# Pairs of heads on both halves of the array, and expert weights in 8 KB runs with a ring of 2048-column tiles

## The chip, the cores and the metric

The kernel runs on one core of one Trainium2 chip. The metric is the device time of one execution in microseconds (us), lower is better. A core has a matrix engine (TensorE, in the profile PE for the products and PEld for the loading of the stationary operand), VectorE (DVE), ScalarE (ACT), GpSimd (POOL) and SyncE (SP), which here issues nearly all DMAs. Sixteen DMA engines carry the data. The profile gives one execution.

## What is computed

Two transformer stacks follow each other on a sequence of 256 tokens of width 1024, in fp32. Weights and all inputs lie in DRAM.

```python
# first block: 4 layers, mixers of three kinds in turn (sparse, dilated, block attention; 12 heads of 64)
x = layer_norm(ALPHA * x + concat([mix, memory_attention]) @ w_out)
x = layer_norm(ALPHA * x + swiglu(x, w_gate_up, w_down))
# second block: 2 layers; layer 0 mixes with rwkv7 and spatial gating, layer 1 with latent attention (16 heads)
h = layer_norm_2(DN_ALPHA * h + mix)
h = layer_norm_2(DN_ALPHA * h + mem_cross_attention(h, mem))
h = layer_norm_2(DN_ALPHA * h + hier_moe(h))      # 32 experts, 2 of them for a token
# an expert: silu(x @ w_gate[e]) * (x @ w_up[e]) @ w_down[e], [1024, 512], [1024, 512], [512, 1024]
```

In the first block the mixers have queries, keys and values of 64 columns a head; memory attention has four such heads over 256 memory rows. All 32 experts' weights are read for each of the two layers, 402.7 MB of the 697 MB that the kernel moves.

## The kernel before

**Order of the work.** The program is written in order and a planner of the framework lays out each engine's instructions from it by a simulated timeline; waits on buffers and data are put in by the framework. So instructions of neighbouring steps can change places on an engine, while the order in which buffers go round is that of the program.

**Attention.** 256 tokens are two row blocks `t`. A head's query and key are transposed, so that its 64 columns lie in 64 partitions: even heads in partitions 0 to 63, odd heads in 64 to 127. A score product thus uses one half of the rows of the matrix array. `softmax_T` (L484) takes heads of one half, as many as fit into a PSUM bank of 512 columns, into one bank (`at`, two banks in all): products (L495), mask and maximum on DVE (L497), exponential with sum on ACT (L503), division on DVE (L508), then `prob_T` with transposes on PE (L517) and a copy on ACT (L519). `attn_plain` (layers 0, 2 and 3; L526) calls it for the even heads, multiplies the result with v (L548), and goes on with the odd heads. The output of a head has 64 rows, so a product with v uses one half of the array's columns. `attn_dilated` (layer 1; scores L571, transposes L587, v L597) takes head by head; `attn_mem` (all four layers; scores L611, v L618) again the even heads and then the odd ones, the scores directly through `softmax_full`. In the second block `mla` has heads of 96 partitions (also L495) and products with v (L1426) whose column half changes from head to head. A product of fp32 operands leaves two records in the trace.

**Projections.** `unit` loads raw weights in tiles of 1 MiB (`raw`), ACT copies them rounded into a tile `wh` (L283), GpSimd or, in places, DVE writes the rest into `wl` (L285), and `mac` (L300 to L302) or `projT` (L329 to L331) multiplies both. The pairs `wh`, `wl` of 512 columns come from a ring (`wtiles`, L239): twelve pairs in the first block, four in the first part of the second (pool `wp`, `NWP = 4`), eight from its first output projection on (`wp` and `wx`). A pair is free when its last product is done. `lag` (L247) sets how far the second row block's products trail, by the number of pairs.

**Experts.** The 32 experts of a layer are taken in eight groups of four (`moe_group`); each has 32 places, so a group's activations fill 128 columns. A group needs 24 tiles of 1 MiB (gate, up and down, eight each). `moe_sources` (L1742) lists them: a tile holds two experts, and of each two neighbouring rows of 512 columns (gate, up) or one row of 1024 columns (down), 4 KB in one run. In the last group the down tiles hold four experts' 512-column halves. `moe_prefetch` (from L1777) puts tiles wherever memory is free at the time, in a round of 18 (layer 0) or 20 tiles (layer 1): `own` (tile `spill`), `mem`, `mraw`, `kv`, `xT`, `raw`, and four "w" tiles, each made of two pairs of the weight ring; `moe_fill` (L1758) then loads four pieces of 512 columns into `wh` and `wl` of both pairs, as four DMAs with runs of 2 KB (L1766), and whole tiles otherwise (L1768). `products` (L1828) asks for the tiles of a step and multiplies: for gate and up two tiles, each with two experts and two of eight row chunks; the four experts write 32 rows of a bank each, so that they use a quarter of the array's columns each (L1841). The selection of the tokens is L1824, the sum into the output L1593. After group 0 the program branches on a count (`overflow`, L1644, L1645): a further round for experts with more than 32 tokens.

Of the kernel before, what the change touches and what calls it, by code (L numbers as in the profile page):

```python
# [34 lines left out]
class K:  # L35
# [187 lines left out]
    def weight_rings(self, *rings):  # L223

        self.wslots = [p for p, n in rings for _ in range(n)]
        self.wcount = dict(rings)
        self.wnext = 0
# [162 lines left out]
class First(K):  # L390
# [96 lines left out]
    def softmax_T(self, t, heads, mask, W, scale=SCALE):  # L487

        nc = self.nc
        n = len(heads)  # L490
        p = self.at((128, 512 // W, W))
        s = self.s_tile()[:, :512].rearrange("p (j w) -> p j w", w=W)
        mx = self.sm(n, tag="amx", pad=4)
        for j, (q, k) in enumerate(heads):
            nc.tensor.matmul(p[:, j, :], q, k, start=True, stop=True)  # L495
        for j in range(n):
            nc.vector.tensor_tensor_reduce(out=s[:, j, :], in0=p[:, j, :], in1=mask, scale=1.0, scalar=SENT,  # L497
                                           op0=OP.add, op1=OP.max, accum_out=mx[:, j:j + 1])
        nm = self.sm(n, tag="anm", pad=4)
        nc.vector.tensor_scalar(nm, mx, -scale, None, op0=OP.mult)  # L500
        sums = self.sm(n, tag="asums", pad=4)
        for j in range(n):
            nc.scalar.activation(out=s[:, j, :], in_=s[:, j, :], func=AF.Exp, bias=nm[:, j:j + 1], scale=scale,  # L503
                                 accum_out=sums[:, j:j + 1])
        rs = self.sm(n, tag="ars", pad=4)
        nc.vector.reciprocal(rs, sums)
        for j in range(n):
            nc.vector.tensor_scalar(s[:, j, :], s[:, j, :], rs[:, j:j + 1], None, op0=OP.mult)  # L508
        return self.prob_T(s, n, W)

    def prob_T(self, s, n, W):
# [8 lines left out]
        return PT  # L520

# [8 lines left out]
    def attn_plain(self, t, qkT, vt, mask, mixT):  # L530
# [6 lines left out]
        for b0 in range(0, 12, 8):  # L537
            oT = self.mm((128, 4, 128))
            hmax = min(12, b0 + 8)
            for h0 in range(b0, hmax, 2 * per):  # L540
                for par in range(2):
                    hs = list(range(h0 + par, min(hmax, h0 + 2 * per), 2))
                    r = slice(64 * par, 64 * par + 64)
                    PT = self.softmax_T(t, [(qkT[r, h // 2, t * 128:(t + 1) * 128], qkT[r, 6 + h // 2, 0:W]) for h in hs],
                                        mask, W)
                    for j, h in enumerate(hs):
                        for kt in range(nk):
                            nc.tensor.matmul(oT[r, (h // 2) % 4, :], vt[kt][:, h * 64:h * 64 + 64],  # L548
                                             PT[:, j * nk + kt, :], start=(kt == 0), stop=(kt == t))
# [4 lines left out]
    def attn_dilated(self, t, qkT, vt, mixT):  # L554
# [3 lines left out]
        for h in range(4):  # L558
            heads = []
            for g in range(3):  # L560
                hh = 4 * g + h
                r = slice(64 * (hh % 2), 64 * (hh % 2) + 64)
                heads.append((qkT[r, hh // 2, t * 128:(t + 1) * 128], qkT[r, 6 + hh // 2, 0:W]))
            s = self.s_tile()[:, :3 * W].rearrange("p (g w) -> p g w", g=3)
            mx = self.sm(3, tag="amx", pad=4)
            per = 512 // W
            p = None
# [1414 lines left out]
```

## Time and profile before

| | us |
|---|---|
| median of 3 timed runs (2998.13 to 3003.35) | 2998.79 |
| profiled execution | 2996.07 |
| its span, first to last instruction | 2994.2 |
| PE busy | 2661.2 (89%) |
| DVE busy | 1415.1 (47%) |
| GpSimd busy | 1023.5 (34%) |
| ACT busy | 905.3 (30%) |

Busy time of PE is that of its pipelined products, whose ends are modelled. The page cuts the span into 40 equal slices of 75 us; a digit is the busy share in tenths, and the line of GB/s is what the DMA engines moved. Where PE stands at 9 the matrix work sets the pace; where the GB/s stay at one high level, the transfers do. First block: 0 to about 1400 us; second block's layer 0: mixer and attention to about 1840, experts to 2310; layer 1: to 2517, experts to 2980.

### The profile page before, as it was taken

How to read it: one execution, taken by the hardware profiler on the slowest of the kernel's cores; microseconds unless marked ns; L12 is line 12 of the kernel's file. 1: busy time of each engine (PE TensorE's matmuls, PEld its weight loads, DVE VectorE, ACT ScalarE, POOL GpSimd, SP SyncE). 2: the span in 40 equal slices, each digit the busy share in tenths (PEclk: the TensorE clock that was granted, in tenths of full speed). 3: DMA queues.
4: the chain of work that ended last, by engine and by line, in shares of the span. 5: the costliest groups of instructions: out<-in, count | busy, mean ns of one | idle time of the engine just before them, and what ended most of it. 6: DMA issues, size and time to landing. Idle time of an engine off the chain costs nothing. (4 is left out here: it accounts for less than half of the span.)

```text
span 2994.2 us, 37225 instructions
## 1 busy us (share of the span) xinstructions
PE 2661.2 (89%) x13571; PEld 1845.7 (62%) x13571; DVE 1415.1 (47%) x3091; ACT 905.3 (30%) x1760; POOL 1023.5 (34%) x809
## 2 busy tenths in 40 slices
PE   6899999999999999999899989877786999877885
PEld 5678876888778877887788866322331776322321
DVE  8766554765566576666775664100101654100011
ACT  3454453554555435553432041000000641000000
POOL 6445571656545572655454140000000440000000
PEclk8899997999999999999999999999998999999998
DMA  6335552555445542555433167999999367999997
GB/s 203 112 125 188 180 197 71 179 187 187 142 139 194 183 161 98 169 192 168 141 101 99 71 238 273 376 403 405 403 404 390 128 229 292 368 406 403 406 403 305
DMA packets 271579, 697.48 MB, mean 233 GB/s; under 512 B 16666, under 2 KB 47504, under 8 KB 271376
## 3 DMA queue, kind: packets, MB, share of 16 engines
q1 hardware_dynamic: 265616, 676.59, 62.4%
q0 software_dynamic: 5760, 18.32, 1.8%
q8 instruction: 111, 1.82, 0.3%
q14 instruction: 92, 0.75, 0.1%
HBM read 693.80 MB, written 1.05 MB: 232 GB/s over the span
## 5 line engine op out<-in xcount | busy, mean ns | idle before, releaser
L285 POOL TENSOR_TENSOR wl<-raw,wh 128x512 fp32r<-128x512 f32 (+3 forms) x680 | 929.8, 1392 | 1314.8 <-ACT wh L283 1275.3
L283 ACT ACTIVATE wh<-raw 128x512 fp32r<-128x512 f32 (+3 forms) x972 | 596.9, 626 | 566.8 <-PE mm L301 267.9
L300 PE MATMUL mm<-wh,xh 128*128 128x512 f32 (+3 forms) x1352 | 531.8, 396 | 13.9 <-DVE w L92 8.4
L301 PE MATMUL mm<-wh,xl 128*128 128x512 f32 (+3 forms) x1352 | 526.1, 390 | 0.2
L302 PE MATMUL mm<-wl,xh 128*128 128x512 f32 (+3 forms) x1352 | 520.5, 389 | 0.0
L285 DVE TENSOR_TENSOR wl<-raw,wh 128x512 fp32r<-128x512 f32 x292 | 398.9, 1388 | 162.2 <-PE mm L301 89.8
L300 PEld LDWEIGHTS mm<-wh,xh 128*128 128x128 f32 x1352 | 260.3, 193 | 66.7 <-ACT cs L454 8.8
L301 PEld LDWEIGHTS mm<-wh,xl 128*128 128x128 f32 x1352 | 260.5, 193 | 50.6 <-DVE xl L151 2.1
L302 PEld LDWEIGHTS mm<-wl,xh 128*128 128x128 f32 x1352 | 258.7, 191 | 50.0 <-issue 0.5
L1849 ACT ACTIVATE w<-at 128x512 f32<-128x512 f32 x16 | 9.6, 597 | 847.1 <-PE at L1841 847.1
L1639 POOL TENSOR_TENSOR x<-x,gb 128x512 f32<-128x512 f32 x2 | 3.5, 1726 | 482.9 <-DVE x L1638 482.9
L1824 PEld LDWEIGHTS tp<-oh,x 128*128 128x128 f32 x512 | 125.9, 334 | 41.8 <-issue 26.5
L1824 PE MATMUL tp<-oh,x 128*128 128x128 f32 x512 | 133.9, 413 | 12.9 <-PEq L1645 9.9
L1851 DVE SCALAR_TENSOR_TENSOR w<-w,at 128x512 f32<-128x512 f32 x16 | 11.0, 688 | 262.7 <-PE at L1841 262.7
L300 PE MATMUL mm<-wh,big 128*128 128x512 f32 x352 | 134.4, 391 | 0.0
L301 PE MATMUL mm<-wh,big 128*128 128x512 f32 x352 | 133.2, 389 | 0.0
L1850 DVE SCALAR_TENSOR_TENSOR w<-w,at 128x512 f32<-128x512 f32 x16 | 11.0, 687 | 255.7 <-ACT w L1849 255.7
L302 PE MATMUL mm<-wl,big 128*128 128x512 f32 x352 | 127.1, 390 | 0.0
L1841 PE MATMUL at<-mraw,xg 128*32 128x512 f32 x432 | 90.1, 644 | 40.5 <-DMA mraw<-in_moe_w_up_dram 23.5
L1841 PE MATMUL at<-raw,xg 128*32 128x512 f32 x328 | 70.5, 661 | 26.9 <-DMA raw<-in_moe_w_up_dram 17.8
L1841 PE MATMUL at<-xh,xg 128*32 128x512 f32 x200 | 57.7, 695 | 33.5 <-DMA xh<-in_moe_w_gate_dram 16.9
L1841 PE MATMUL at<-xl,xg 128*32 128x512 f32 x240 | 69.5, 668 | 12.3 <-DMA xl<-in_moe_w_gate_dram 7.0
(579 smaller groups left out, 4239.6 us busy)
## 6 DMA issues: line engine op xcount, KB each, us to landing
raw<-in_w_gate_up_dram SPq DMA_DIRECT2D x80, 1024.0 KB, 5.2
raw<-in_w_down_dram SPq DMA_DIRECT2D x44, 1024.0 KB, 4.9
mraw<-in_moe_w_down_dram SPq DMA_DIRECT2D x31, 1024.0 KB, 18.4
mraw<-in_moe_w_gate_dram SPq DMA_DIRECT2D x28, 1024.0 KB, 18.1
raw<-in_moe_w_up_dram SPq DMA_DIRECT2D x26, 1024.0 KB, 12.9
mraw<-in_moe_w_up_dram SPq DMA_DIRECT2D x26, 1024.0 KB, 18.4
raw<-in_w_in_a_dram SPq DMA_DIRECT2D x22, 1024.0 KB, 5.2
raw<-in_moe_w_down_dram SPq DMA_DIRECT2D x19, 1024.0 KB, 12.9
```

Of the source, the lines that this page charges most:

```text
L283: nc.scalar.activation(out=hi, in_=src, func=AF.Copy)
L285: (nc.vector if on_dve else nc.gpsimd).tensor_tensor(lo, src, hi.bitcast(F32), op=OP.subtract)
L300: nc.tensor.matmul(p, xh, hi[:, a:b], start=first, stop=False)
L301: nc.tensor.matmul(p, xl, hi[:, a:b], start=False, stop=False)
L302: nc.tensor.matmul(p, xh, lo[:, a:b], start=False, stop=last)
L1639: (nc.vector if t else nc.gpsimd).tensor_tensor(xs[t][:, s], xs[t][:, s], b[:, s], op=OP.add)
L1824: nc.tensor.matmul(p[:, j, :], xs[t].rearrange("p (q k) -> p k q", k=8)[:, kc, :], O[t], start=(t == 0), stop=(t == 1))
L1841: nc.tensor.matmul(p[ss, :], x[:, ss], got[u][m * i + j], start=first, stop=last, tile_position=(0, s0))
L1849: nc.scalar.activation(out=h, in_=gu[0], func=AF.Tanh, scale=0.5)
L1850: nc.vector.scalar_tensor_tensor(h, h, 1.0, gu[0], op0=OP.add, op1=OP.mult)
L1851: nc.vector.scalar_tensor_tensor(h, h, 0.5, gu[1], op0=OP.mult, op1=OP.mult)
```

## The change

Three things are changed. In attention, the scores of a pair of calls (even and odd heads) are issued in turn into two banks (`scores`), and the products with v in turn as well (`weighted`); both softmaxes are between them. `attn_plain`, `attn_dilated` and `attn_mem` use both, `mla` only `weighted`. The weight ring of the second block hands out tiles `wq` of 2048 columns (`wquad`), each holding two pairs; the memory is the same, half as many tiles. An expert tile holds one expert, and of it four rows of 512 or two of 1024 columns, which lie next to each other in DRAM: 8 KB in one run. So a step of `products` takes four tiles with one expert each, and a "w" tile is one whole `wq` tile with one DMA. The last group's down tiles keep their layout.

```diff
-    def weight_rings(self, *rings):
+    def weight_rings(self, *rings, paired=False):
+        self.wpaired = paired
...
+        if self.wpaired:
+            if self.wnext % 2 == 0:
+                self.wtwo = self.wquad()
+            self.wnext += 1
+            return self.weight_views(self.wtwo)[1 - self.wnext % 2]
...
+    def wquad(self):
+        p = self.wslots[self.wnext % len(self.wslots)]
+        return p.tile([128, 4 * WCOLS], F32R, tag="wq", name="wq", bufs=self.wcount[p] // 2)
...
+    def scores(self, groups, W):
+        banks = [self.at((128, 512 // W, W)) for _ in groups]
+        for j in range(len(groups[0])):
+            for p, heads in zip(banks, groups):
+                self.nc.tensor.matmul(p[:, j, :], *heads[j], start=True, stop=True)
+        return banks
+
+    def softmax_T(self, groups, mask, W, scale=SCALE):
+        nc = self.nc
+        n = len(groups[0])
+        banks = self.scores(groups, W)
+        res = []
+        for p in banks:
...
+            res.append((s, sums))
+        return [self.prob_T(self.divided(s, sums, n), n, W) for s, sums in res]
...
+    def weighted(self, steps, nk):
+        for js in steps:
+            for kt in range(nk):
+                for out, v, P in js:
+                    self.nc.tensor.matmul(out, v(kt), P(kt), start=(kt == 0), stop=(kt == nk - 1))
...
-                for par in range(2):
-                    hs = list(range(h0 + par, min(hmax, h0 + 2 * per), 2))
-                    r = slice(64 * par, 64 * par + 64)
-                    PT = self.softmax_T(t, [(qkT[r, h // 2, t * 128:(t + 1) * 128], qkT[r, 6 + h // 2, 0:W]) for h in hs],
-                                        mask, W)
...
+                cs = range(h0 // 2, min(hmax, h0 + 2 * per) // 2)
+                rows = [slice(0, 64), slice(64, 128)]
+                PT = self.softmax_T([[(qkT[r, c, t * 128:(t + 1) * 128], qkT[r, 6 + c, 0:W]) for c in cs] for r in rows],
+                                    mask, W)
+                self.weighted([[(oT[r, c % 4, :], lambda kt, h=2 * c + par: vt[kt][:, h * 64:h * 64 + 64],
+                                 lambda kt, j=j, P=PT[par]: P[:, j * nk + kt, :]) for par, r in enumerate(rows)]
+                               for j, c in enumerate(cs)], nk)
...
-        pairs = [slice(gi * EG + e, gi * EG + e + 2) for e in range(0, EG, 2)]
+        ones = [slice(gi * EG + e, gi * EG + e + 1) for e in range(EG)]
         for n in ("moe_w_gate", "moe_w_up"):
-            w = A[n][l].rearrange("e (p q k) n -> q p e (k n)", q=4, k=2)
-            yield from (w[q][:, es, :] for q in range(4) for es in pairs)
-        w = A["moe_w_down"][l].rearrange("e (p k) n -> k p e n", k=4)
+            w = A[n][l].rearrange("e (p q k) n -> q p e (k n)", q=2, k=4)
+            yield from (w[q][:, es, :] for q in range(2) for es in ones)
         if gi < NG - 1:
-            yield from (w[k][:, es, :] for k in range(4) for es in pairs)
+            w = A["moe_w_down"][l].rearrange("e (p q k) n -> q p e (k n)", q=2, k=2)
+            yield from (w[q][:, es, :] for q in range(2) for es in ones)
         else:
+            w = A["moe_w_down"][l].rearrange("e (p k) n -> k p e n", k=4)
...
-                got = [[t.bitcast(F32) for _ in range(1024 // WCOLS) for t in self.wtiles()]]
+                got = [[self.wquad().bitcast(F32)]]
+                self.wnext += 2
...
-            for k in range(0, 8, 2):
-                products([(p, xg[:, k + j, :], k + j == 0, k + j == 7) for j in range(2)])
+            for k in range(0, 8, 4):
+                products([(p, xg[:, k + j, :], k + j == 0, k + j == 7) for j in range(4)])
...
-            for k in range(4):
-                products([(yp[n], hT[:, k, :], k == 0, k == 3) for n in ns])
+            for k in range(0, 4, len(ns)):
+                products([(yp[n], hT[:, k + j, :], k + j == 0, k + j == 3) for j in range(len(ns)) for n in ns])
...
-            self.weight_rings((wp, NWP))
+            self.weight_rings((wp, NWP), paired=True)
...
-                    self.weight_rings((wp, NWP), (wx, NWP))
+                    self.weight_rings((wp, NWP), (wx, NWP), paired=True)
```

## Rows read from the trace of the kernel before

**Rows 1.** The page by 40 slices: PE's busy tenths, and GB/s moved.
```profile
PE   6899999999999999999899989877786999877885
...
GB/s 203 112 125 188 180 197 71 179 187 187 142 139 194 183 161 98 169 192 168 141 101 99 71 238 273 376 403 405 403 404 390 128 229 292 368 406 403 406 403 305
```

**Rows 2.** Busy time by stretch: PE, PEld, DVE, ACT, POOL, clock, DMA share, GB/s.
```profile
1400.00:1740.00 340.00, 311.76 (x2074) 274.33 (x2073) 234.41 (x535) 101.17 (x174) 145.21 (x120) 0.95 0.36 117
...
1915.00:2308.00 393.00, 305.70 (x1473) 103.67 (x1472) 37.47 (x67) 3.58 (x6) 0.00 (x0) 0.97 1.03 402
...
2584.00:2978.00 394.00, 313.62 (x1484) 106.75 (x1484) 37.99 (x68) 3.58 (x6) 0.00 (x0) 0.94 1.02 397
```

**Rows 3.** The same view, 4 us each: 4 KB runs, then twice 2 KB runs.
```profile
2031.00:2035.00 4.00, 2.88 (x16) 0.53 (x16) 0.00 (x0) 0.00 (x0) 0.00 (x0) 1.00 1.03 410
...
2107.00:2111.00 4.00, 4.00 (x20) 1.91 (x16) 0.00 (x0) 0.00 (x0) 0.00 (x0) 1.00 1.05 389
2657.00:2661.00 4.00, 4.00 (x18) 1.88 (x14) 1.19 (x3) 0.00 (x0) 0.00 (x0) 1.00 1.05 388
```

**Rows 4.** DMA issues: count, KB each, us to landing; as many go to `wl`.
```profile
wh<-in_moe_w_up_dram SPq DMA_DIRECT2D x60, 256.0 KB, 7.0
...
wh<-in_moe_w_gate_dram SPq DMA_DIRECT2D x56, 256.0 KB, 9.3
...
wh<-in_moe_w_down_dram SPq DMA_DIRECT2D x42, 256.0 KB, 7.4
```

**Rows 5.** The page's count of DMA packets by size.
```profile
DMA packets 271579, 697.48 MB, mean 233 GB/s; under 512 B 16666, under 2 KB 47504, under 8 KB 271376
```

**Rows 6.** Timeline of SP at layer 0's branch: start, us, queue, line, what.
```profile
1891.58 2.31 SPq L1768 DMA_DIRECT2D mraw<-in_moe_w_down_dram  x1
1910.57 0.38 SPq L1768 DMA_DIRECT2D spill<-in_moe_w_gate_dram  x1
```

**Rows 7.** Timeline of PE in layer 0's attention: start, us, records.
```profile
158.30 0.72 PE L495 MATMUL at<-big 64*128 64x128 f32 x8
...
163.52 1.13 PE L495 MATMUL at<-big 64*128 64x256 f32 x4 [0.36 <-DVE amx L497]
...
165.53 1.62 PE L495 MATMUL at<-big 64*128 64x256 f32 x8
...
169.88 1.09 PE L548 MATMUL mm<-big 128*64 128x128 f32 x8
```

**Rows 8.** Timeline of PE in the latent attention: products with v.
```profile
2378.77 0.66 PE L1426 MATMUL mm<-ring,vv 128*64 128x128 f32 x8
```

**Rows 9.** Groups by line: busy us, mean ns; idle before, and what ended it.
```profile
L548 PE MATMUL mm<-big 128*64 128x128 f32 x216 | 29.4, 280 | 5.5 <-ACT big L519 5.5
L495 PE MATMUL at<-big 64*128 64x256 f32 (+1 forms) x144 | 24.2, 356 | 1.7 <-DVE big L92 1.1 <-DVE amx L497 0.5
L618 PE MATMUL mm<-big,mv 128*64 128x128 f32 x128 | 21.9, 326 | 0.7 <-ACT big L519 0.7
L611 PE MATMUL at<-mkT,big 64*128 64x256 f32 x64 | 20.3, 469 | 10.1 <-ACT big L631 9.8 <-ACT w L822 0.2
L571 PE MATMUL at<-big 64*128 64x128 f32 (+1 forms) x48 | 15.6, 500 | 3.9 <-DVE amx L572 3.6
```

**Rows 10.** Busy time by stretch: the end of layer 0's attention.
```profile
157.30:179.40 22.10, 19.08 (x133) 14.23 (x131) 17.66 (x74) 17.05 (x51) 2.38 (x2) 1.00 0.44 144
```

**Rows 11.** Groups by line, 1400 to 1850 us: the two steps of weight conversion.
```profile
L283 ACT ACTIVATE wh<-raw 128x512 fp32r<-128x512 f32 x136 | 84.0, 630 | 171.5 <-PE mm L330 66.5 <-PE mm L301 63.4 <-issue 28.0
...
L285 POOL TENSOR_TENSOR wl<-raw,wh 128x512 fp32r<-128x512 f32 x112 | 149.1, 1352 | 150.1 <-ACT wh L283 133.5 <-PE mm L302 13.5 <-issue 2.2
```

**Rows 12.** PE's waits, 1400 to 1850 us: total, times, longest; the largest for weights.
```profile
PE mm L302 <- POOL xh L285: 2.1, 2, 1.9
```

**Rows 13.** Busy time by stretch: one expert group of layer 1.
```profile
2586.00:2648.00 62.00, 46.91 (x229) 15.78 (x225) 5.46 (x11) 0.60 (x1) 0.00 (x0) 0.97 1.03 404
```

**Rows 14.** DVE's groups by shape, layer 0's attention: mask and maximum of a head.
```profile
L497 DVE CUSTOM_DVE_ANT_0 big<-at,am 128x256 f32<-128x256 f32 x12 | 4.6, 418 | 0.1
```

More of the change, by code (lines that the diff above doesn't have):

```diff
@@ new lines, in attn_dilated @@
+        per = 512 // W
+        ts = slice(t * 128, t * 128 + 128)
+        for h0 in range(0, 4, 2):
+            rows = [slice(0, 64), slice(64, 128)]
+            s = [self.s_tile()[:, :3 * W].rearrange("p (g w) -> p g w", g=3) for _ in rows]
+            mx = [self.sm(3, tag="amx", pad=4) for _ in rows]
+            for g0 in range(0, 3, per):
+                gs = range(g0, min(3, g0 + per))
+                cs = [2 * g + h0 // 2 for g in gs]
+                banks = self.scores([[(qkT[r, c, ts], qkT[r, 6 + c, 0:W]) for c in cs] for r in rows], W)
+                for i, p in enumerate(banks):
+                    for g in gs:
+                        nc.vector.tensor_tensor_reduce(out=s[i][:, g, :], in0=p[:, g - g0, :], in1=masks[g], scale=1.0,
+                                                       scalar=SENT, op0=OP.add, op1=OP.max, accum_out=mx[i][:, g:g + 1])
+            PT = [self.dilated_T(s[i], mx[i], t, W) for i in range(2)]
+            oT = self.mm((128, 4, 128))
+            parts = []
+            for r0 in range(h0 * 192, h0 * 192 + 384, 64):
+                ch, ro = divmod(r0, 128)
+                parts.append((oT[ro:ro + 64, ch % 3, :], lambda kt, r0=r0: vt[kt][:, r0:r0 + 64],
+                              lambda kt, P=PT[r0 // 192 - h0]: P[:, kt, :]))
+            self.weighted([parts[i:i + 2] for i in range(0, 6, 2)], t + 1)
+            c0 = 3 * (h0 // 2)
+            self.split(mixT[0][:, c0:c0 + 3, ts], mixT[1][:, c0:c0 + 3, ts], oT[:, 0:3, :])
@@ new lines, in dilated_T @@
+    def dilated_T(self, s, mx, t, W):
+        nc = self.nc
+        nm = self.sm(1, tag="anm", pad=4)
+        nc.vector.tensor_reduce(nm, mx, axis=AX.X, op=OP.max, negate=True)
+        nc.vector.tensor_scalar(nm, nm, SCALE, None, op0=OP.mult)
+        sm = self.sm(1, tag="asums", pad=4)
+        nc.scalar.activation(out=s, in_=s, func=AF.Exp, bias=nm, scale=SCALE, accum_out=sm)
+        rs = self.sm(1, tag="ars", pad=4)
+        nc.vector.reciprocal(rs, sm)
+        P = s[:, 0, :]
+        nc.vector.tensor_tensor(P, P, s[:, 1, :], op=OP.add)
+        nc.vector.tensor_tensor(P, P, s[:, 2, :], op=OP.add)
+        nc.vector.tensor_scalar(P, P, rs, None, op0=OP.mult)
+        tp = self.tp((128, 4, 128))
+        for kt in range(t + 1):
+            nc.tensor.transpose(tp[:, kt, :], P[:, kt * 128:(kt + 1) * 128], self.ident)
+        PT = self.pt_tile().rearrange("p (j w) -> p j w", w=128)
+        nc.scalar.activation(out=PT[:, :t + 1, :], in_=tp[:, :t + 1, :], func=AF.Copy)
+        return PT
```

117 lines of the change are left out of this document (30 added, 87 removed).

## Prediction, before the changed kernel was built or run

> **What bounds the kernel now.** I read the page by slices first, for where the kernel changes its limit. PE is at 9 tenths in nearly every slice up to two thirds of the span; then the transfers run at about 405 GB/s for two long blocks while PE falls to 7 or 8 tenths [rows 1]. The reader is to see two kernels in one: matrix work first, expert weights afterwards. The busy time by stretch settles it. From 1915 to 2308 us and from 2584 to 2978 us the DMA engines are busy all the time (a share of 1.02 to 1.03) at 402 and 397 GB/s, and PE works 306 and 314 of 393 and 394 us [rows 2]. So 787 us are paced by how fast expert weights arrive, and only faster arrival shortens them. In the matrix part, 1400 to 1740 us for one, PE works 312 of 340 us and the transfers reach 117 GB/s: there only less work or less waiting on PE counts [rows 2].
>
> **Part 1: expert weights in 8 KB runs.** Each tile of 1 MiB has 128 partitions of 8 KB. Before, such a row comes as two runs of 4 KB (two experts), or, in the tiles that lie in the weight ring, as four runs of 2 KB in four DMAs of 256 KB [rows 4]. After, it is one run of 8 KB, and one DMA. Three stretches of 4 us show the price of a run: where only 4 KB runs were under way, 410 GB/s; where only 2 KB runs were, 389 and 388 [rows 3]. A MiB (1.0486 MB) takes 1.0486/0.410 = 2.558 us by the one and 1.0486/0.388 = 2.703 us by the other. Each of the 16 engines moves 16 runs of 4 KB or 32 runs of 2 KB in that time: 159.8 and 84.5 ns each. So 2 KB more in a run cost 75.3 ns, and a run has some 9 ns of its own. Continued to 8 KB: 159.8 + 2 x 75.3 = 310.4 ns, eight of them 2.483 us, 422 GB/s. A tile gains 0.075 us against 4 KB runs and 0.220 us against 2 KB runs. This is an extrapolation by a factor of two, and the step on which most hangs.
>
> How many tiles: 393 us at 402 and 394 us at 397 GB/s are 314.4 MB or 300 tiles. The last group's eight down tiles of each layer stay in 2 KB runs, so 284 change. Of all 384 tiles, (60 + 56 + 42) / 2 = 79 went to the ring, 21% [rows 4]; of 284 that is 60. The sum is 60 x 0.220 + 224 x 0.075 = 13.2 + 16.8 = 30 us. Some tiles before these stretches gain too, but there SP issues nothing from 1893.9 to 1910.6 us, where the program branches, and the queue runs dry [rows 6]; what arrives earlier there waits, and I count 2 us for it, 32 in all. SP itself saves three of four issues per ring tile; in the steady state it stands in its own full queue (2.31 us in one issue [rows 6], about a tile's time), so that is free. Bounds: 9 us, if 8 KB runs keep the pace of 4 KB ones (60 x 0.145), to 37 us, if the earlier tiles count in full.
>
> PE now needs four tiles for a step instead of two. It runs the first pieces of the first three while it waits for the fourth, and the expert stretch from 2586 to 2648 us, one group's time, holds 46.9 us of PE work in 62 [rows 13]. A group's 24 tiles take at least 59 us after the change. I cost this at nothing, covered by those 12 us; what it costs without the cover is the third rival.
>
> **Part 2: two heads of different array halves together.** Before, the heads of one half are done, then those of the other. The timeline shows both cases, because the planned order sometimes already put two calls side by side: eight score records of 128 columns took 0.72 us, while four records of 256 columns in one half took 1.13 us alone and eight of them 1.62 us where two calls met only in part [rows 7]. For the products with v, eight records in one column half took 1.09 us [rows 7]; in the latent attention, where the halves come in turn by head, eight took 0.66 us [rows 8]. So the pairing works on this engine: a factor of 0.61 for v, and for 256-column scores about 1.2 us instead of 2 x 1.13.
>
> Plain attention (three layers): the v products hold 29.4 us and the scores 24.2 us [rows 9]. At 0.61 the first give 11.5 us; the scores, partly paired already, about 5: 16 us. But in the stretch from 157.3 to 179.4 us PE works 19.1, DVE 17.7 and ACT 17.1 of 22.1 us [rows 10]. With PE shorter, DVE is late next, and 22.1 - 17.7 = 4.4 us is the most that a layer can give; I take 3, so 9 in all. Memory attention (eight calls): 21.9 us of v products and 20.3 us of scores [rows 9], at 0.61 and 0.53 a saving of 8.5 + 9.5 = 18. It lies among projections that keep PE full, so PE time saved is time saved, but before these scores PE also stood idle 10.1 us for a bank, which stays. I take 10. Dilated attention: 15.6 us of scores [rows 9], partly paired; I take 2, with 0 and 8 as bounds. Latent attention changes only the order within a pair of v products: 1. The sum is 22 us, with 9 + 18 + 8 + 1 + 4 = 40 as the upper bound (the 4 is 3 x 4.4 less the 9).
>
> Its cost: a pair of calls needs both score banks free at once. PE then waits until DVE has masked what the second bank held: two reductions of 418 ns and their read-outs, about 1.0 us [rows 14]. There are some 29 such pairs (15 plain, 8 memory, 6 dilated), so 29 us is the bound on the loss side if nothing else is queued on PE; I take none, since projections stand behind most of these pairs and the bank was waited for before, too. The Trainium skill, page "TensorEngine Tiling (Array Packing)", section "Restrictions and Gotchas", says that different row tiles can't access one PSUM bank at the same time, so sharing one bank between the halves would not be a way around this wait.
>
> **Part 3: a ring of 2048-column tiles.** In the second half of the model four (later eight) slots become two (later four) tiles that each hold two weight pairs, and a tile is refilled only when both pairs are used up. ACT's copy into a free tile takes 630 ns, GpSimd's rest behind it 1352 ns [rows 11]; 136 pairs, 68 tiles, pass there. Queued behind a late copy on ACT are the copies of the next pairs, and PE waits for them. With single slots PE waited for weights in four places, the largest sum of 2.1 us [rows 12], at most 8.4 in all, because ACT waits 66.5 + 63.4 us for PE instead [rows 11]: the ring is full, and PE is late. Lower bound 0 (that slack covers everything); upper bound 68 x (0.63 + 1.35) = 135 us (no overlap at all). I take the value near the row that shows slack: 10 us. It is made of the six 512-column projections through four slots, where the second row block lags by two chunks: there the refill is needed just as the tile comes free, two times 1.3 us each, 16 us, of which other matrix work fills a good third.
>
> **Sum.** Against the profiled run's 2996.07 us (span 2994.2 and 1.9 around it): 2996 - 32 - 22 + 10 = 2952 us. The three timed runs have a median of 2998.79, 2.7 above the profiled run; I shift by a part of that: 2953 us.
>
> **Rivals.**
> First, 8 KB runs go no faster than 4 KB ones. For it: in a profile of 271579 packets only 203 are of 8 KB or more [rows 5], none of them weights, so no row shows the new pace. Against it: the price per byte between 2 and 4 KB is steady. Then only the ring's 60 tiles gain, 9 us: 2996 - 9 - 22 + 10 = 2975. The Trainium skill, page "DMA: Bandwidth & Descriptors", section "SWDGE vs HWDGE vs iDMA", gives a packet as preferably at most 4096 B; if that means that longer runs are cut to this size, it is this rival. The trace bears it out as far as weights go, but packets of more than 8 KB do exist.
> Second, the attention gains nothing, since DVE and ACT end its chain (17.7 and 17.1 of 22.1 us [rows 10]) or the planned order had the halves together anyway: 2996 - 32 + 10 = 2974.
> Third, PE becomes late in the expert stretches: with longer waits the granted clock (0.97 there now [rows 13]) falls to its lower level more often, and 12 us more per group eat the gain: 2996 - 22 + 10 = 2984.
> Fourth, the other side: the ring of two tiles makes PE wait. If each of the 68 refills is late by GpSimd's 1.35 us, that is 92 us: 2996 - 54 + 92 = 3034, slower. It decides from 54/68 = 0.79 us a refill on. Against it: ACT's 130 us of waiting for PE, and other chains' matrix work between the projections.
>
> **How the numbers follow.** The forecast has 0.52; the first rival 0.16, the second 0.14, the third 0.06, the fourth 0.08; 0.04 is left for a new order that evens it all out. A measurement of this kernel tells 0.2%, 6 us, from no change. The first two rivals and most of the third are faster, which with the forecast makes 0.85; 0.07 for no change, 0.08 for slower. The range goes from 2918 (37 and 40 us of gain, no cost) to 2986 (the third rival and a little): it takes in three rivals and leaves out the fourth.
>
> **What would show it.** In the changed profile: transfers at about 422 GB/s in the expert stretches (410 would be the first rival), each some 20 us shorter at most; expert issues of 1024 KB only; v products at about 0.66 us for eight records; the stretch after the first layer's projections about 3 us shorter with DVE nearly full; PE's waits for ACT's and GpSimd's weight copies of about 15 us between 1400 and 1850 us, not 90; and PE's clock in the expert stretches not below about 0.9. The prediction is wrong if the run price doesn't continue to 8 KB, or if a refill of the ring is on PE's path nearly every time.

## The result, and the profile after

The changed kernel takes 2956.6 us (median of 4 runs, 2955.75 to 2962.95) against 2999.19 us before (4 runs); the ratio is 0.986 with a 95% interval of 0.9843 to 0.9877, so 42.6 us less, 36.9 to 47.1 by the interval. The forecast was 2953 us. The profiled execution takes 2956.99 us.

The page by slices (the lines that answer to [rows 1], with the granted clock, and the count of packets that answers to [rows 5]):

```profile
PE   6899999999999998999899989888787899877885
...
PEclk8899998999999999999999999999999999999989
...
GB/s 199 121 116 188 182 199 86 188 182 191 136 145 187 184 161 115 165 177 162 150 86 103 111 164 234 399 422 421 421 421 401 177 179 280 397 421 421 421 422 307
DMA packets 201220, 697.41 MB, mean 236 GB/s; under 512 B 12874, under 2 KB 43712, under 8 KB 153920
```

The two expert blocks stand at 421 GB/s where they stood at 403 to 406. Of 201220 packets, 47300 have 8 KB or more (203 before): the runs arrive whole.

Busy time by stretch of after (us, then PE, PEld, DVE, ACT, GpSimd with their counts, granted clock, DMA share, GB/s): the matrix part of [rows 2], the two expert stretches, one expert group as in [rows 13], and the attention stretch of [rows 10].

```profile
1400.00:1740.00 340.00, 312.11 (x2044) 275.46 (x2043) 225.52 (x510) 90.14 (x163) 140.98 (x114) 0.94 0.34 113
...
1915.00:2250.00 335.00, 270.19 (x1333) 97.75 (x1333) 32.54 (x60) 2.99 (x5) 0.00 (x0) 0.94 1.01 421
2584.00:2910.00 326.00, 260.67 (x1289) 94.17 (x1287) 29.83 (x53) 3.58 (x6) 0.00 (x0) 0.93 1.01 421
...
2586.00:2648.00 62.00, 48.21 (x266) 18.95 (x266) 6.15 (x12) 0.60 (x1) 0.00 (x0) 1.00 1.01 421
...
157.30:179.40 22.10, 18.70 (x113) 12.94 (x113) 15.58 (x72) 15.03 (x47) 0.39 (x1) 0.85 0.41 133
```

In a group's 62 us PE gets through 266 records instead of 229. In the attention stretch it gets through 113 instead of 133, at a clock of 0.85 instead of 1.00: in this execution the change brought nothing there.

Both kernels have 13571 matrix records, so the start of the k-th one, counted from the first, shows where the time went. Time in before, then how far the others are ahead (minus) or behind there (three of the experiments below beside after; one profiled execution each):

```
record   before    after  attention alone  ring alone  e10_split
  2000    464.0     -0.4        -1.6           +0.3       -3.7
  2250    524.6    -10.3       -11.6           +0.3      -10.8
  6300   1399.9    -11.7       -13.0           +0.3      -12.3
  8250   1704.0     -1.4       -13.2          +13.2      -14.4
  9000   1863.7     -4.6       -13.7           +8.4      -17.1
 10750   2328.4    -21.1       -12.0           +3.5      -34.7
 11750   2516.5    -22.5       -10.0           +2.3      -35.8
 13560   2970.2    -38.5        -9.7           -3.0      -51.1
```

Four steps stand out in the column of after: 10 us won within the 60 us of the dilated layer's attention, 10 us lost again in the second block's first mixer (records 6300 to 8250), 16.5 us won in layer 0's experts and 16.0 in layer 1's. The profiled execution of before (2996.07 us) lies at the fast end of its runs (2995 to 3007 us over all that were timed), so differences of profiles come out some 4 us smaller than those of medians.

### The profile page after: what moved, and what is told of

The parts are those of the page before. It is cut to its first block, busy times and chain, and to the rows that moved or that the text cites. A ratio compares the mean times of both kernels' runs of the same rounds, so it can differ in the third digit from the quotient of the medians.

```text
span 2954.8 us, 36636 instructions
## 1 busy us (share of the span) xinstructions
PE 2623.8 (89%) x13571; PEld 1833.6 (62%) x13571; DVE 1418.1 (48%) x3091; ACT 897.8 (30%) x1760; POOL 1024.6 (35%) x809
## 2 busy tenths in 40 slices
DMA packets 201220, 697.41 MB, mean 236 GB/s; under 512 B 12874, under 2 KB 43712, under 8 KB 153920
## 5 line engine op out<-in xcount | busy, mean ns | idle before, releaser
L296 POOL TENSOR_TENSOR wl<-raw,wh 128x512 fp32r<-128x512 f32 (+1 forms) x520 | 724.1, 1418 | 604.4 <-ACT wh L294 588.7
L294 ACT ACTIVATE wh<-raw 128x512 fp32r<-128x512 f32 (+1 forms) x776 | 479.7, 628 | 326.5 <-PE mm L312 183.5
L311 PE MATMUL mm<-wh,xh 128*128 128x512 f32 (+2 forms) x1152 | 454.7, 397 | 12.9 <-DVE w L92 8.9
L296 POOL TENSOR_TENSOR wq<-raw,wq 128x512 fp32r<-128x512 f32 (+2 forms) x160 | 206.5, 1315 | 701.8 <-DMA raw<-in_mla_w_in_dram 459.7
L312 PE MATMUL mm<-wh,xl 128*128 128x512 f32 (+2 forms) x1152 | 449.6, 391 | 0.0
L313 PE MATMUL mm<-wl,xh 128*128 128x512 f32 (+2 forms) x1152 | 448.7, 391 | 0.0
L296 DVE TENSOR_TENSOR wl<-raw,wh 128x512 fp32r<-128x512 f32 x256 | 358.9, 1426 | 143.6 <-PE mm L312 90.1
L294 ACT ACTIVATE wq<-raw 128x512 fp32r<-128x512 f32 (+2 forms) x196 | 109.1, 611 | 247.3 <-issue 117.5
L1869 PE MATMUL at<-mraw,xg 128*32 128x512 f32 x432 | 120.2, 678 | 31.6 <-DMA mraw<-in_moe_w_up_dram 22.7
L1869 PE MATMUL at<-wq,xg 128*32 128x512 f32 x464 | 124.2, 662 | 26.3 <-DMA wq<-in_moe_w_up_dram 17.9
L1869 PE MATMUL at<-xl,xg 128*32 128x512 f32 x240 | 129.0, 672 | 12.8 <-DMA xl<-in_moe_w_gate_dram 8.5
```

What stands on the lines that cost most here:

```text
L294: nc.scalar.activation(out=hi, in_=src, func=AF.Copy)
L296: (nc.vector if on_dve else nc.gpsimd).tensor_tensor(lo, src, hi.bitcast(F32), op=OP.subtract)
L311: nc.tensor.matmul(p, xh, hi[:, a:b], start=first, stop=False)
L312: nc.tensor.matmul(p, xl, hi[:, a:b], start=False, stop=False)
L313: nc.tensor.matmul(p, xh, lo[:, a:b], start=False, stop=last)
L1869: nc.tensor.matmul(p[ss, :], x[:, ss], got[u][m * i + j], start=first, stop=last, tile_position=(0, s0))
```

## The experiments

### Each part alone

The prediction's sum has three parts. Each was added to the kernel before by itself; the other two stayed as they were.

**e1_attn**, the changes of `softmax_T`, `scores`, `weighted` and the four attention functions alone.

> The kernel before with the attention part alone: scores of even and odd heads in turn into two banks, products with v in turn; ring and expert tiles as before. Theory of the prediction: 22 us faster, about 2977, of it 9 in plain, 10 in memory, 2 in dilated and 1 in latent attention. Rival read from the trace of after (its progress by matrix instructions is 11.7 us ahead of before at the end of the first block, 10 of them won between the dilated layer's 464 and 515 us, none in the memory parts): 12 to 15 us faster, about 2985. Second rival: the lead in the first block comes from another order of the planner and not from the pairing: within 6 us of 2999.

Measured: 2983.07 us against 3000.4, ratio 0.9941 (0.9928 to 0.9955): 17 us less. The column above shows them nearly all in one place, the dilated layer.

**e2_runs**, `moe_sources` and the steps of `products` alone.

> The kernel before with the 8 KB runs alone: expert tiles of one expert, four tiles a step, but the ring as before, so that its 'w' tiles still come as four DMAs of 256 KB in 2 KB runs. Theory that the time goes by the length of a run: the 224 tiles outside the ring gain 0.075 us each, 17 us, the ring's 60 nothing: about 2982, and 412 GB/s in the expert stretches. Rival, the gain of after comes from the ring's tiles arriving in one DMA rather than four (fewer and larger DMAs): no gain here, about 2999 at 402 GB/s. Rival, steps of four tiles make PE late: slower than 2999.

Measured: 2986.42 us, ratio 0.9947 (0.9934 to 0.996): 14 us less where the theory of the run's length expected 17, and neither rival holds in full. The expert stretches reach 406 and 408 GB/s, not the expected 412. In the group from 2586 to 2648 us it is 397 GB/s at a DMA share of 0.99, so the transfers were not always kept going there; whether the ring's tiles in 2 KB runs or the steps of four tiles do that is not shown.

**e3_ring**, `wquad`, `paired=True` and the "w" tile as one DMA alone.

> The kernel before with the ring of 2048-column tiles alone: expert tiles of two experts in 4 KB runs as before, a 'w' tile being one ring tile with one DMA, now in 4 KB runs. Theory: the paired release costs 10 us between 1400 and 1700 us (the page after shows a lead of 11.7 us shrink to 1.4 there), and 60 tiles go from 2 KB to 4 KB runs, 9 us less: within 3 us of 2999. Rival, the shrinking lead is a matter of the attention's order or of the granted clock: 9 us faster, about 2990. Rival, the ring costs 92 us: no longer possible after the result.

Measured: 2992.71 us, ratio 0.9974 (0.9963 to 0.9984): 8 us less. That lies between the two expectations, and the table tells where: the ring loses 12.8 us between 1400 and 1700 us, as the first theory said, but about 16 come back, not 9: 13.2 us behind at record 8250, 8.4 at the start of the experts, 3.0 ahead at the end. PE's waits in that stretch (1400 to 1700 us; us in total, times, longest), first of the ring alone, then of after:

```profile
PE mm L342 <- POOL wq L296: 6.2, 13, 0.9
PE mm L340 <- ACT wq L294: 1.1, 1, 1.1
```
```profile
PE mm L342 <- POOL wq L296: 6.1, 13, 0.9
PE mm L340 <- ACT wq L294: 0.7, 1, 0.7
```

L342 is the last product of the transposed projections (L331 before), where PE had waited 1.9 and 1.5 us for `wl`, five times. By the code, `projT` takes a unit of four pairs and goes over all of them twice (f = 0, then 1). With four single slots, the next unit's first pair can be written when two chunks of the second pass are done; with two tiles only after four, and the conversion (ACT's step has a mean of 623 ns, GpSimd's of 1359 ns in after) no longer fits into what is left of the pass. This is read from the code.

These waits are the smaller part of the loss. From record 6300 to 8250, in before and then in after:

```profile
1404.15:1708.40 304.25, 284.17 (x1951) 253.25 (x1950) 207.07 (x440) 89.70 (x152) 137.32 (x112) 0.97 0.36 117
```
```profile
1392.75:1707.25 314.50, 291.32 (x1951) 258.50 (x1950) 208.38 (x440) 84.02 (x152) 138.06 (x112) 0.95 0.35 113
```

The stretch is 10.2 us longer, but PE stands idle only 3.1 us more (23.2 instead of 20.1). The other 7.2 us are PE's busy time for as many records, at a mean granted clock of 0.95 instead of 0.97. The ring alone and e8_4k, which have the same two tiles, also show 0.95 there; the attention part alone has 0.97 and e10_split 0.98. What makes the clock fall with the ring, the waits or the other order, is not shown.

### The length of a run

**e8_4k**, after with tiles of two experts again:

```diff
-            w = A[n][l].rearrange("e (p q k) n -> q p e (k n)", q=2, k=4)
+            w = A[n][l].rearrange("e (p q k) n -> q p e (k n)", q=4, k=2)
...
-            for k in range(0, 8, 4):
+            for k in range(0, 8, 2):
```

> The kernel after with expert tiles of two experts again, 4 KB in a run and two tiles a step; attention and ring as in after, a 'w' tile still one DMA. Theory that time goes by the length of a run: 410 GB/s in the expert stretches instead of 421, 284 tiles x 0.07 us = 20 us slower than after, about 2977. Rival, fewer and larger DMAs are what counts: as fast as after, 2957.

Measured: 2979.33 us, ratio to before 0.9933 (0.9919 to 0.9947), 22.7 us more than after. Tiles, DMAs and their size are those of after; only the run is half as long. The same two stretches:

```profile
1915.00:2250.00 335.00, 267.33 (x1296) 92.23 (x1296) 31.62 (x59) 2.98 (x5) 0.00 (x0) 0.94 1.03 409
2584.00:2910.00 326.00, 260.00 (x1260) 90.50 (x1258) 30.25 (x54) 2.98 (x5) 0.00 (x0) 0.94 1.03 409
```

409 to 421 GB/s is 1.0486 x (1/0.409 - 1/0.421) = 0.073 us a tile, 20.8 us for 284. It is the length of the run that counts. PE's clock is the same within 0.01, so it has no part in this.

### The ring

**e10_split**, after with single pairs in the first part, and one pool of four tiles from the first output projection on:

```diff
+            self.kv = ctx.enter_context(pool("kv"))
-            wp = ctx.enter_context(pool("wp"))
-            self.weight_rings((wp, NWP), paired=True)
+            first = ExitStack()
+            wp = first.enter_context(pool("wp"))
+            self.weight_rings((wp, NWP))
...
-                    self.weight_rings((wp, NWP), (wx, NWP), paired=True)
+                    first.close()
+                    self.weight_rings((wx, 2 * NWP), paired=True)
```

> The kernel after, with the weight ring of the second block's first part in single pairs of 512 columns again (four, in a pool that is closed when the later ring opens), and the later ring of four 2048-column tiles in one pool. Expert tiles and their 8 KB runs stay. Theory that the paired release of two tiles costs the 10 us between 1417 and 1700 us (e3_ring lost 12.8 us there by itself), and that with four tiles it costs nothing: 2946. Rival, the four tiles cost as much, or the new pool has to wait: 2954 to 2960.

Measured: 2948.05 us (2945.49 to 2951.44, 5 runs), ratio to before 0.9832 (0.9819 to 0.9845), against 0.986 for after: 8.5 us less than after by the medians, and the slowest of its runs is faster than the fastest of after. Between records 6300 and 8250 of the table nothing is lost any more (12.3 us ahead, then 14.4). PE's waits there are those of before again:

```profile
PE mm L342 <- POOL wl L296: 1.5, 3, 0.6
PE mm L342 <- DVE wl L296: 1.4, 2, 1.0
```

PE's busy time from record 6300 to 8250 is 281.6 us, less than before. So the two tiles cost what was lost there, by the waits and by the clock, and four tiles cost nothing that can be seen.

**e9_kept** tried the same in another way: a ring tile is kept for good while projections go round, and its two pairs are overwritten one by one.

```diff
-            if self.wnext % 2 == 0:
-                self.wtwo = self.wquad()
+            if i not in self.wkept:
+                self.wkept[i] = self.wquad()
```

> The kernel after, but a 2048-column ring tile is kept while projections go round and only handed over anew for an expert tile; so a pair is overwritten as soon as its own products are done, while an expert tile still arrives as one DMA in 8 KB runs. Theory that the paired release costs 8 to 10 us in the second block's first mixer: about 2947, and the waits of the transposed projections for GpSimd's rest (6.1 us in 13 between 1400 and 1850 us) go back to about 1.5. Rival, those 10 us come from the planner's order or from the clock there (0.91 against 0.96 in 1400 to 1480 us): within 3 us of 2956.

Measured: 2951.82 us, ratio 0.9838 (0.9825 to 0.985). The number decides nothing: the program asks for a unit's four pairs before the trailing row block's products with the last two pairs of the unit ahead stand in it; with a tile handed out anew they keep their own weights, with a kept tile they read the next unit's. So a part of the products is done with other weights, and with other dependences.

### The attention

**e5_dilated**, **e6_plain**, **e7_memory**: pairs of heads in one of the three functions alone, in the kernel before. The others keep the order of before, for plain attention for instance by

```diff
+                for par, r in enumerate([slice(0, 64), slice(64, 128)]):
+                    P1, = self.softmax_T([[(qkT[r, c, t * 128:(t + 1) * 128], qkT[r, 6 + c, 0:W]) for c in cs]], mask, W)
+                    self.weighted([[(oT[r, c % 4, :], lambda kt, h=2 * c + par: vt[kt][:, h * 64:h * 64 + 64],
+                                     lambda kt, j=j: P1[:, j * nk + kt, :])] for j, c in enumerate(cs)], nk)
```

> The kernel before with pairs of heads in dilated attention alone (and the turn within a pair of v products in latent attention, about 1 us); plain and memory attention as before. The prediction gave dilated attention 2 us (bounds 0 and 8). Theory now: dilated attention holds most of the 17 us that the attention part alone brought, since in the trace of before the matrix engine runs at a granted clock of 0.5 from 495 to 510 us there and the section is 10 us shorter in after: about 2989. Rival, the whole attention part is needed: within 6 us of 3000.

> The kernel before with pairs of heads in plain attention alone (layers 0, 2 and 3); dilated and memory attention as before. The prediction gave it 9 us: about 2991. Theory now: the matrix engine has less to do per softmax and falls to the lower clock in this very stretch (granted 0.50 from 170 to 175 us in after and from 165 to 170 us in the attention part alone, 1.00 all through in before), which takes the gain back: 0 to 4 us faster, about 2998.

> The kernel before with pairs of heads in memory attention alone (all four layers); plain and dilated as before. The prediction gave it 10 us, because it lies among projections that keep the matrix engine full: about 2990. Theory now: the work saved (8.7 us of v products) returns as waiting for the score banks (14.2 us idle ahead of these scores in after, 10.1 in before) and as other order: 0 to 4 us faster, about 2998.

Measured: dilated 2986.58 us, ratio 0.9954 (0.994 to 0.9967), 14 us less; plain 2998.05, 0.9992 (0.9982 to 1.0002); memory 2999.44, 0.9998 (0.9988 to 1.0008). So 14 of the 17 us come from dilated attention; the other two can't be told from nothing.

What the clock did, for plain attention: PE's busy time by stretch in layer 0, of plain alone, then of after, then of e8_4k. Before, the whole section had 1.00 [rows 10].

```profile
165.00:170.00 5.00, 5.00 (x15) 2.91 (x15) 2.78 (x17) 3.19 (x12) 0.00 (x0) 0.50 0.00 1
170.00:175.00 5.00, 5.00 (x26) 3.21 (x23) 4.06 (x20) 5.00 (x16) 0.00 (x0) 0.62 0.00 0
```
```profile
165.00:170.00 5.00, 2.91 (x21) 1.94 (x19) 5.00 (x25) 5.00 (x17) 0.00 (x0) 0.96 0.00 0
170.00:175.00 5.00, 4.97 (x26) 3.58 (x26) 3.05 (x10) 3.30 (x12) 0.00 (x0) 0.50 0.52 150
175.00:180.00 5.00, 5.00 (x33) 3.57 (x32) 0.69 (x1) 2.26 (x4) 0.00 (x0) 0.85 0.18 65
```
```profile
170.00:175.00 5.00, 3.48 (x30) 2.48 (x30) 3.84 (x11) 4.55 (x14) 0.00 (x0) 1.00 0.33 86
```

A granted 0.50 is the lower of TensorE's two levels, 1.2 GHz. The order of the records doesn't settle it: after, e8_4k and e10_split have the same first 800 matrix records in the same order (by name and shape), up to beyond this section, and in the last two the clock stays at 1.00 from 140 to 205 us. Their profiles show what plain attention gains when the clock doesn't fall. Layer 0's section (records 560 to 760) in before, in e8_4k and in after:

```profile
154.85:191.90 37.05, 34.03 (x201) 26.31 (x200) 21.07 (x79) 19.46 (x55) 4.83 (x3) 1.00 0.26 86
```
```profile
153.60:189.55 35.95, 31.83 (x202) 23.97 (x201) 21.05 (x79) 19.29 (x55) 4.87 (x3) 1.00 0.28 89
```
```profile
152.85:190.85 38.00, 34.60 (x201) 25.80 (x200) 21.00 (x79) 19.26 (x55) 4.84 (x3) 0.91 0.27 84
```

Layer 2's (records 3560 to 3760) in before and in plain alone:

```profile
817.60:853.70 36.10, 34.61 (x202) 26.79 (x201) 20.60 (x68) 18.98 (x49) 4.69 (x4) 1.00 0.28 89
```
```profile
819.30:854.55 35.25, 32.93 (x201) 24.54 (x200) 20.45 (x68) 19.14 (x49) 4.68 (x4) 1.00 0.29 91
```

PE's work falls by 2.2 and 1.7 us, the section by 1.1 and 0.9: about half of what PE saves comes back as waiting for the softmax's other steps, at full clock. Where the clock falls, layer 0's section takes 37.3 to 38.0 us (attention part alone, plain alone, after), and the rest of the gain is gone too.

The pairing itself works, as the timeline of after in this stretch shows (start, us, records): sixteen v records in 1.31 us at full clock, 0.66 for eight; but fourteen in 1.97 where the clock is low.

```profile
156.95 1.31 PE L552 MATMUL mm<-big 128*64 128x128 f32 x16
158.71 1.55 PE L504 MATMUL at<-big 64*128 64x256 f32 x8 [0.45 <-DVE amx L517]
...
171.76 1.97 PE L552 MATMUL mm<-big 128*64 128x128 f32 x14
```

Memory attention is a different matter. The groups of after (busy, mean ns, idle before):

```profile
L504 PE MATMUL at<-mkT,big 64*128 64x256 f32 x64 | 20.6, 526 | 14.2 <-ACT big L659 13.9 <-ACT w L850 0.2
L552 PE MATMUL mm<-big,mv 128*64 128x128 f32 x128 | 13.2, 291 | 0.9 <-ACT big L543 0.9
```

The v products fall from 21.9 to 13.2 us [rows 9], a factor of 0.60; the scores stay at 20.3 to 20.6, and PE waits 4 us longer for a bank. The scores of layer 0, first before, then after:

```profile
119.84 1.13 PE L611 MATMUL at<-mkT,big 64*128 64x256 f32 x4
125.91 2.98 PE L611 MATMUL at<-mkT,big 64*128 64x256 f32 x8 [4.36 <-ACT big L631]
```
```profile
119.91 1.13 PE L504 MATMUL at<-mkT,big 64*128 64x256 f32 x4
125.96 2.99 PE L504 MATMUL at<-mkT,big 64*128 64x256 f32 x8 [4.33 <-ACT big L659]
```

They are laid out as before: the program has them in turn, but the planner still puts the four of one bank ahead of the four of the other. In layers 1 and 2 the first row block's do come in turn, but the second's run in part at the lower clock. Layer 1, one line of each row block, before and then after:

```profile
439.03 1.13 PE L611 MATMUL at<-mkT,big 64*128 64x256 f32 x4
443.57 1.13 PE L611 MATMUL at<-mkT,big 64*128 64x256 f32 x4 [1.17 <-ACT big L631]
```
```profile
438.02 0.70 PE L504 MATMUL at<-mkT,big 64*128 64x256 f32 x4
443.78 2.07 PE L504 MATMUL at<-mkT,big 64*128 64x256 f32 x4 [3.25 <-ACT big L659]
```

So the unchanged sum of 20.3 to 20.6 us hides a gain and a loss.

**e11_in_turn** keeps the two heads side by side and takes the turns out of the program:

```diff
-        for j in range(len(groups[0])):
-            for p, heads in zip(banks, groups):
+        for p, heads in zip(banks, groups):
+            for j in range(len(groups[0])):
...
-            for kt in range(nk):
-                for out, v, P in js:
+        for i in range(len(steps[0])):
+            for js in steps:
+                out, v, P = js[i]
+                for kt in range(nk):
```

> The attention part alone (e1_attn), with the two heads still taken together into two banks and their softmaxes side by side, but the products not in turn: all scores of the even heads, then all of the odd ones, and the v products likewise, even heads first. Theory that the halves of the array working at the same time bring the gain: most of the 17 us is gone, 2992 to 3000. Rival, the gain is that two heads are in flight while the other engines work on one, so that the matrix engine waits less and keeps its clock: still 12 to 17 us faster than before, 2983 to 2988.

Measured: 2989.03 us, ratio 0.9966 (0.9954 to 0.9978), 12 us less than before: between the two, nearer to the rival. Dilated attention by stretch, in before, in the attention part alone (e1_attn), and in this kernel:

```profile
485.00:513.00 28.00, 25.00 (x109) 15.73 (x107) 21.17 (x90) 11.63 (x29) 2.20 (x2) 0.60 0.27 82
```
```profile
485.00:513.00 28.00, 24.24 (x130) 17.41 (x130) 14.15 (x62) 9.73 (x22) 0.00 (x0) 0.82 0.24 79
```
```profile
485.00:513.00 28.00, 23.60 (x142) 17.04 (x140) 16.52 (x70) 10.29 (x25) 1.51 (x1) 1.00 0.34 112
```

Before, this stretch ran at a mean granted clock of 0.60. With two heads in flight and no turns in the program it ran at 1.00, and this kernel wins 10.3 us on before from record 2000 to 2250. (In its trace some records of the two halves still start together, two at 464.79 us for instance.) With the turns it wins 10.0 there, at 0.82. So the program's turns are not needed for those 10 us. But the kernels also differ in clock. The whole section (records 2000 to 2250) in before, in after, in e8_4k, whose records there have the order of after, and in this kernel:

```profile
468.50:529.15 60.65, 57.65 (x252) 41.40 (x251) 30.77 (x110) 20.52 (x45) 7.59 (x6) 0.76 0.18 60
```
```profile
468.45:519.15 50.70, 46.57 (x252) 34.86 (x251) 30.00 (x113) 21.35 (x47) 7.58 (x6) 0.90 0.27 93
```
```profile
466.00:519.50 53.50, 49.52 (x252) 36.66 (x251) 30.11 (x113) 21.25 (x47) 7.57 (x6) 0.84 0.26 88
```
```profile
469.10:519.40 50.30, 45.90 (x252) 34.96 (x251) 29.88 (x111) 20.84 (x46) 7.59 (x6) 1.00 0.24 83
```

In one and the same order, 0.06 of clock makes 2.8 us. By that price, an estimate, 0.76 to 0.90 makes some 6 of the 10 us between before and after, and the order with turns would take some 46 us at 1.00, 4 less than the one without. So most of the dilated layer's gain is a higher clock; that the turns are worth something at an equal clock is likely, but no run shows it. The 6 us between the two medians can't be placed: the profiles are 3 us apart, and 2.3 of that stand at record 2000 already, ahead of the dilated layer.

**e13_twice**, to ask whether more work on PE keeps the clock up in plain attention:

```diff
+        for _ in range(times):
+            for j in range(len(groups[0])):
+                for p, heads in zip(banks, groups):
...
-                                    mask, W)
+                                    mask, W, times=2)
```

> The attention part alone (e1_attn), with every score product of plain attention issued twice, the second time over the first with the same result: added work for the matrix engine, some 12 us at full clock in three layers if the halves work together, and nothing else changed. Theory that plain attention loses its gain to the lower clock: the stretch from 155 to 185 us keeps a granted clock near 1.0, and the added work costs little, 2980 to 2987 (e1_attn: 2983). Rival, the clock there has nothing to do with how busy the engine is: the lower clock stays and the run is 8 to 14 us slower than e1_attn, 2991 to 2997.

Measured: 3015.43 us, ratio 1.0045 (1.0031 to 1.0058), 32 us slower than e1_attn and worse than the rival said. The theory has fallen:

```profile
155.00:160.00 5.00, 2.28 (x17) 1.58 (x15) 5.00 (x13) 1.82 (x3) 3.60 (x3) 1.00 0.62 189
160.00:190.00 30.00, 29.96 (x106) 22.09 (x107) 14.81 (x82) 14.25 (x53) 0.00 (x0) 0.50 0.12 39
```

After 2.76 us of waiting for DVE the clock is at its lower level for 30 us in which PE is busy all the time. Waiting alone isn't it either: before, PE worked 2.98 of the 5 us from 170 to 175 us, and the clock stayed at 1.00. Nor is the order alone: one order had both clocks (after and e8_4k above). What lets it fall in these sections stays open.

**e12_split_dilated** is e10_split with plain attention in the order of before, as in the diff above, and memory attention too:

```diff
-        banks = self.scores([[(qmT[r, j, t * 128:(t + 1) * 128], mkT[r, j, :]) for j in range(2)] for r in rows], 256)
-        PT = []
-        for p in banks:
+        for par, r in enumerate(rows):
+            p, = self.scores([[(qmT[r, j, t * 128:(t + 1) * 128], mkT[r, j, :]) for j in range(2)]], 256)
...
```

> e10_split (8 KB runs, single pairs in the first ring) with plain and memory attention head by head as before, so that only dilated attention takes heads in pairs. Theory that plain and memory attention together bring 3 us or less: 2948 to 2953. Rival, they bring the 19 us of the prediction: 2967.

Measured: 2948.2 us (2942.91 to 2951.65), ratio 0.9822 (0.9809 to 0.9836): as fast as e10_split. By their medians both are 8 us faster than the changed kernel.

## Why the prediction came out right, step by step

**What bounds the kernel: right.** The expert stretches gained with the pace of the transfers, 16.5 and 16.0 us, and the matrix part only where PE worked or waited less. One thing is missing in it: the granted clock changes what the same work costs there, and it moved both the dilated layer and the second block's first mixer by several us.

**8 KB runs: right.** Forecast 422 GB/s and 2.483 us a tile. SP's queue shows it directly, an issue every 2.48 us (timeline of SP in after):

```profile
2617.83 0.33 SPq L1793 DMA_DIRECT2D wq<-in_moe_w_gate_dram  x1
2620.32 0.33 SPq L1793 DMA_DIRECT2D xh<-in_moe_w_gate_dram  x1
2622.80 0.33 SPq L1793 DMA_DIRECT2D xl<-in_moe_w_gate_dram  x1
```

The extrapolation of 75 ns for every 2 KB of a run held at twice the length. The sum was 32 us; the trace has 32.5 in the two expert blocks (16.5 and 16.0). The first rival is out (e8_4k is slower than after by 22.7 us). The Trainium skill, page "DMA: Bandwidth & Descriptors", section "SWDGE vs HWDGE vs iDMA", gives a packet as at most 4096 B preferably, in a table on what GpSimd builds for its own DMAs. The loads here are issued by SyncE; their packets of 8 KB arrived whole and went faster, 421 against 409 GB/s, so for these loads the measurement decides against that preference.

**Pairs of heads: the sum nearly right (22 forecast, 17 measured), its terms wrong.** Plain attention was given 9 us and brought 2 or nothing. The step that failed is that PE's shorter work would end the stretch earlier, up to DVE's 17.7 us, by 3 us a layer. At full clock the sections of layers 0 and 2 got 1.1 and 0.9 us shorter for 2.2 and 1.7 us less work: the rest came back as waits in the chain of a softmax, which DVE's busy time doesn't show. In after and two other kernels the clock also fell in layer 0, which the row of before at 1.00 [rows 10] couldn't show; e8_4k and e10_split show that it need not. Memory attention was given 10 and brought 1 or nothing: its v products shrank as forecast (0.60 against 0.61), its scores not at all in sum, because the planner kept the old order in layers 0 and 3 and part of the others ran at the lower clock, and PE waited 4 us longer for banks, a wait that was costed at nothing. Eight score records of 256 columns in turn took 1.40 to 1.55 us at full clock, not the 1.2 of the prediction. Dilated attention was given 2 and brought 14: the mean of 500 ns a record [rows 9] was read as the price of the work, though much of it ran at the lower clock. With two heads in flight the clock was higher, with the turns (0.90 over the section) and without them in the program (1.00, e11_in_turn); by the estimate above some 6 of the 10 us there are the clock's, a term the prediction didn't have.

**The ring: the size right (10 forecast, 10.3 in after, 12.8 alone), by luck.** The forecast was some 15 us of PE waiting for the copies in the projections of 512 columns, a third of it filled. PE's waits for the copies come to 7.8 us (6.1 + 1.0 + 0.7, 1400 to 1850 us), where before had 6.5 (2.1 + 1.9 + 1.5 + 1.0), and most of them lie in the transposed projections. All of PE's idle time grew by 3.1 us; the other 7.2 are busy time of as many records at a lower mean clock, which the prediction had no term for. The argument that ACT's 130 us of waiting for PE are slack was no protection: in after ACT still stands idle 46.5 and 16.0 us for PE there, and PE waits for GpSimd all the same, at the places where the next unit begins. Slack summed over a stretch doesn't say where it lies.

**The other rivals.** PE is not late in the expert stretches: the clock there is 0.94 and 0.93, and PE waits for transfers. The ring cost time, as the fourth rival said, but 10 us in all, not 92; that is 0.15 us a refill, far from the 0.79 at which it decides. The second rival, an attention that gains nothing, is true of two of its three functions. Of the signs named beforehand one failed with it: layer 0's section did not get 3 us shorter (38.0 us in after, 37.05 before), and DVE worked 21.0 us of it.

**The sum.** The forecast was 32 + 22 - 10 = 44 us. By the runs, the attention alone is 17.3, the ring with its single DMA 7.7, and the step from 4 to 8 KB 22.7, together 47.7 where the whole is 42.6; with intervals of some 4 us on each, that difference can't be resolved. So the forecast is right for one large term that was well founded; the three terms of the attention and the ring came out near their sum by errors that cancelled, which is luck.

## What to carry to other kernels

Where transfers pace a stretch, fit the price of a run from stretches with one length each, and lengthen the runs: the line held up to 8 KB. Before a mean duration of matrix records is used as a price, look at the granted clock of that stretch; a gain or a loss there may be that of the clock. One profile of a kernel is not enough for that: the same order of records had the lower clock in one kernel and the full clock in another. A ring of few large tiles frees its slots late in just the loops that go over a whole unit twice; give such loops single slots, and hand out the large tiles only where the large transfers need them.

## What was not expected of the hardware

PE's clock can stay at 0.50 for 30 us while PE is busy for 29.96 of them (e13_twice: scores and v products on half of the array, transposes between them), and be at 1.00 in a stretch of 28 us where it works 23.6 (e11_in_turn). And the same matrix records in the same order had 0.50 from 170 to 175 us in after, and 1.00 in e8_4k and e10_split. So here neither PE's busy time nor the order of its work tells by itself which of the two levels it gets.
